# A decoder layer in float32 on one core: the fast-matmul block sums of both feed-forward layers reordered, and transfers regrouped where each turns to its second matmul

## The chip, the cores and the metric

One core of a Trainium2 chip runs the whole layer. The metric is device time in microseconds (us) of one execution; the time before is the median of three timed runs. One further execution was profiled, and its trace is what the rows below come from.

## What is computed

A decoder layer on 1024 tokens of width 1024, all in float32: a gated feed-forward layer, two attentions side by side, a second gated feed-forward layer, and a gated embedding. Only the feed-forward layers matter here. Cut to them:

```
def swiglu(h, w_gate, w_up, w_down):
    return (silu(h @ w_gate) * (h @ w_up)) @ w_down

x = x + 0.5 * swiglu(rms_norm(x, ffn1_norm), ffn1_w_gate, ffn1_w_up, ffn1_w_down)
...
x = x + 0.5 * swiglu(rms_norm(x, ffn2_norm), ffn2_w_gate, ffn2_w_up, ffn2_w_down)
```

The hidden width is 2816.

## The kernel before

**Precision.** A float32 operand is split into a rounded part "hi" (a cast on ScalarE, L102) and a remainder "lo" (a subtraction on VectorE, L103); `split` records both. A matmul of two such operands is three passes: hi by hi, hi by lo, lo by hi. So a product of 128 x 512 outputs over 512 inputs is 12 matmuls on TensorE, four a pass, and its second pass needs the lo of the activations, its third the lo of the weights.

**The first matmul of a feed-forward layer** (`ffn`) runs over 22 weight blocks n, gate and up in turn, of 256 hidden columns. Block 0 is multiplied in the plain way (`plain`, L251, 24 matmuls for each of 2 x 2 outputs). From n = 1 on, seven products take the place of eight (Winograd's scheme): tokens are halved into `N[0]` and `N[1]`, features into two halves, and the activations are the blocks B[1], B[2] (tokens of `N[0]`), "12" and B[3] (tokens of `N[1]`). The scheme needs four block sums of them: B[5] = "12" - B[1], called T1; B[6] = B[3] - B[5], called T2; B[7] = B[3] - "12", called T3; B[4] = B[2] - B[6]. Each is built in four tiles q of 128 tokens:

- `combo_a(q)` (L363) transposes tile q of `N[1]` on TensorE, copies it to a work tile `w` (L373, L374) and splits it into "12" and B[3].
- `combo_t(q)` (L379) makes T3, T1 and T2 of tile q with four subtractions on VectorE (L387 to L390) and splits T1 into B[5].
- `combo_s(q, m)` splits T2 into B[6] (m = 6) or T3 into B[7] (m = 7).
- `combo_d(q)` (L402) makes the sum for B[4] with two operations on GpSimd (L405, L406); `combo_e(q)` splits it.

`prep(n, m)` splits the weight operand of product (n, m), `sums` and `last_sum` make the weight sums on GpSimd (L268 to L273), `product` records the 12 matmuls (L300), `evict` moves the result.

**The order** is written out by hand. Inside `ffn` a manual schedule is on: every engine executes its instructions in the order of the code, so an instruction that waits holds up all that stand behind it on its engine. `first_entry` and `second_entry` order the start of the two layers, and both end in `products`; then comes the list `seqn`: (1,5), (2,1), (1,6), (2,2), (1,7), (2,6), (2,5), (1,4), (1,3), and so on. (1,5) needs all of B[5], (1,6) all of B[6], (1,7) B[7], (1,4) B[4].

**The first norm.** `first_entry` normalises the four tiles of `N[0]` one after the other: sum of squares (`norm_stat`, ScalarE, then two small operations on GpSimd, L181, L182), scaling (`norm_mul`, VectorE, L185), and transposes with splits (`norm_post`, TensorE, L190).

**The second matmul** (`down`, L494) adds 21 steps (c, i) of three chunks c, i = 0 to 6 being the seven products again. A step is 48 matmuls in the first chunk. Its operands come from DRAM through SyncE's queue: `load_hid(c, i)` loads a sum of the hidden values (two transfers of 512 KB, tile names GF and RN, KH and KL, or Q and Q in turn), `wd_block` loads weights, `load_resid` loads the residual rows X, in two halves of four transfers each. `prep_down(c, i)` splits both operands into four H tiles (four hold two steps), and `evict_down` adds the result to X on VectorE (L499). `prep_down(c, 1)` loads half of the next chunk's weights (names WH, and RAW or WL). "The turn" below is the passage from the first matmul to the second.

Of the kernel before, what the change touches and what calls it, by code (L numbers as in the profile page):

```python
# [35 lines left out]
def tile_hybrid_decoder_layer(  # L36
# [176 lines left out]
    def ffn(N, wg, wu, wd, next_gain, resid, hid, tags, entry, tail):  # L213
# [37 lines left out]
        def plain(f_, half):  # L251

            ps = bank(("pt", "pf")[f_])
            i = 0
            for kh in range(2):
                hl, rb = hls[0, ((1, 2), (5, 4))[f_][kh]], B[("12", 3)[kh]] if half else N[0]["B"][kh]
                for a, b in ((0, 0), (0, 1), (1, 0)):
                    for k in range(4):
                        pe(nc.tensor.matmul(ps[:], hl[:, a, k, :], right(rb, b, k), start=(i == 0), stop=(i == 23)))
# [3 lines left out]
            nc.scalar.activation(E[0][f_][:, half, :], ps[:], AF.Silu)
# [94 lines left out]
            nc.sync.dma_start(hid[j, :, 5:7, :], s34[:])  # L358
            del E[n], E[n - 1]

        C = {"w": {}, "t3": {}}

        def combo_a(q):  # L363

            h = N[1]["h"][q]
            cs = slice(q * P, (q + 1) * P)
            if q == 0:
                B[1], B[2] = N[0]["B"]
                B[3] = [slot("T", [P, 2, 512], F32R) for _ in range(4)]
                B["12"] = slot("X", [P, 2, 4, 512], F32R)  # L370
            w = C["w"][q] = slot(tags["w"][q], [P, 2, 4, P])
            v12, v22 = (turn(h, b, bank(cyc("t", ("pf", "av", "pf", "sc")))) for b in range(2))
            nc.scalar.copy(w[:, 0], v12)  # L373
# [4 lines left out]

        def combo_t(q):  # L379

            cs = slice(q * P, (q + 1) * P)
# [5 lines left out]
            nc.vector.tensor_sub(t3, w[:, 1], w[:, 0])  # L387
            nc.vector.tensor_sub(w[:, 0], w[:, 0], f(B[1][:, 0, :, cs]))
            nc.vector.tensor_sub(w[:, 0], w[:, 0], f(B[1][:, 1, :, cs]))
# [12 lines left out]

# [674 lines left out]
    def first_entry(F):  # L1077
# [13 lines left out]
        for t in range(4):
            norm_stat(N[0], t, ("PT", "WL")[t % 2])
            if t:
                norm_mul(N[0], t - 1)
                norm_post(N[0], t - 1, ps2)
# [12 lines left out]
        F["plain"](0, 0)
        F["a"](0)
        norm_mul(N[1], 2)  # L1110
        norm_mul(N[1], 3)
        F["a"](1)
        products(F)

    def products(F):
# [2 lines left out]
        F["prep"](1, 1)
        F["plain"](1, 0)
        F["a"](2)  # L1120
        F["prep"](1, 2)
# [7 lines left out]
        F["t"](1)
        F["s"](0, 7)  # L1130
        F["s"](1, 7)
        F["d"](0)
# [190 lines left out]
```

## Time and profile before

| | us |
|---|---|
| median of 3 runs | 2404.04 (2401.22 to 2408.77) |
| profiled execution | 2400.58 |
| its span | 2398.9 |
| TensorE busy in it | 2298.9 (96%) |
| VectorE, ScalarE, GpSimd busy | 1463.7, 983.9, 872.1 |
| TensorE busy in 0 to 20 | 5.88 |
| TensorE busy in 60 to 80 | 10.46 |
| TensorE busy in 500 to 520 | 14.51 |
| TensorE busy in 1660 to 1680 | 6.79 |
| TensorE busy in 2100 to 2120 | 14.11 |

In a row of the timeline stand: start, length from the start of the first to the end of the last, engine, line, operation, output and input tiles, form, count, and in brackets the idle time of the engine just before with what ended it. PE is TensorE, DVE VectorE, ACT ScalarE, POOL GpSimd, SPq the queue of SyncE that issues transfers. In a row of the waits stand the waiting engine and line, what it waited for, the sum in us, how often, and the longest. The granted clock (PEclk) is a share of TensorE's full speed. Tile names in the profile lack numbers, so many rows read "H" or "PT".

### The profile page before, as it was taken

To read this page: it belongs to the slowest core of one execution; us is meant where nothing else is said; L and a number is where in the kernel's file an instruction comes from. 1 tells how busy PE (TensorE), PEld (TensorE's weight loads), DVE (VectorE), ACT (ScalarE), POOL (GpSimd) and SP (SyncE) were. 2 spreads that over 40 slices of the span, in tenths; PEclk is the share of its full clock that TensorE was granted. 3 is DMA by queue.
4 is the path that set the end of the run, shared out by engine and by line. 5 is a ranking of instruction groups with operands and counts; after the bars stand their busy time and mean duration, and the time that the engine had idled before them with its cause. 6 is when DMAs were issued, how large, how long until landed. Compare 5 with 4: busy or idle time off the path is not lost.

```text
span 2398.9 us, 32295 instructions
## 1 busy us (share of the span) xinstructions
PE 2298.9 (96%) x12238; PEld 1972.5 (82%) x12238; DVE 1463.7 (61%) x2171; ACT 983.9 (41%) x1753; POOL 872.1 (36%) x752
## 2 busy tenths in 40 slices
PE   6899999989999999999988989997999999989999
PEld 5688888878888999988877877896888888878899
DVE  6754545577773656655665576547555455767763
ACT  5433333333352556544544554334333333333441
POOL 3444535300043556544454343104354453300031
PEclk9899999999999999999999999998999999999999
DMA  4222323373332122322213344432232332654232
GB/s 141 75 99 99 128 79 123 138 298 121 132 115 71 50 75 80 84 63 60 71 50 108 127 133 130 129 123 79 97 119 92 106 116 91 232 221 145 82 121 73
DMA packets 197500, 268.52 MB, mean 112 GB/s; under 512 B 27352, under 2 KB 130776, under 8 KB 197344
## 3 DMA queue, kind: packets, MB, share of 16 engines
q1 hardware_dynamic: 197344, 266.45, 33.3%
q8 instruction: 96, 1.57, 0.3%
q14 instruction: 60, 0.49, 0.1%
HBM read 188.78 MB, written 69.24 MB: 108 GB/s over the span
## 4 chain that ended last, share of the span: by engine, by line
PE 82%; DVE 8%; DMA 4%; ACT 2%; issue 2%; POOL 0%; SPq 0%; DVEq 0%; ACTq 0%; POOLq 0%
PE ps L300 33%; PE ps L494 13%; PE ps L595 11%; PE ps L603 9%; PE ps L1199 4%; PE ps L1051 3%; PE ps L876 3%; PE ps L858 2%; DVE H L103 1%; DVE RN L838 1%; PE ps L820 1%; PE ps L819 1%; DMA RN<-hidden 1%; DMA Q<-hidden 1%; DMA WL<-in_ffn_w_down_dram 1%
## 5 line engine op out<-in xcount | busy, mean ns | idle before, releaser
L494 PE MATMUL ps<-H,H 128*128 128x512 f32 x1848 | 427.6, 393 | 12.9 <-ACT H L102 11.4
L494 PEld LDWEIGHTS ps<-H,H 128*128 128x128 f32 x1848 | 349.6, 190 | 88.2 <-ACT H L102 13.1
L300 PE MATMUL ps<-H,WL 128*128 128x512 f32 x1008 | 243.4, 393 | 0.0
L300 PEld LDWEIGHTS ps<-H,WL 128*128 128x128 f32 x1008 | 189.7, 188 | 42.5
L603 PE MATMUL ps<-H,WH 128*128 128x512 f32 x768 | 212.8, 405 | 5.5 <-ACT PT L749 2.7
L129 POOL TENSOR_TENSOR WL<-RAW,WH 128x512 fp32r<-128x512 f32 (+1 forms) x112 | 130.4, 1188 | 167.7 <-ACT WH L123 129.8
L595 PE MATMUL ps<-WH,H 128*128 128x256 f32 (+1 forms) x1152 | 164.5, 285 | 4.0 <-DVE X L103 3.1
L603 PEld LDWEIGHTS ps<-H,WH 128*128 128x128 f32 x768 | 139.0, 191 | 30.0 <-ACT PT L749 2.9
L595 PEld LDWEIGHTS ps<-WH,H 128*128 128x128 f32 x1152 | 148.1, 189 | 6.2 <-DVE X L103 3.8
L129 POOL TENSOR_TENSOR WL<-Y,WH 128x528 fp32r<-128x528 f32 (+1 forms) x8 | 11.1, 1418 | 378.8 <-PE ps L494 189.6
L103 DVE TENSOR_TENSOR PT<-ps,PT 128x512 fp32r<-128x512 f32 (+1 forms) x160 | 100.4, 633 | 74.9 <-ACT PT L102 74.2
L300 PE MATMUL ps<-H,Q 128*128 128x512 f32 x600 | 143.4, 389 | 0.0
L499 DVE SCALAR_TENSOR_TENSOR X<-ps,X 128x512 f32<-128x512 f32 x168 | 109.0, 684 | 52.8 <-PE ps L494 52.8
L102 ACT CAST PT<-ps 128x512 fp32r<-128x512 f32 (+1 forms) x160 | 87.0, 546 | 111.7 <-PE ps L858 101.5
L300 PEld LDWEIGHTS ps<-H,Q 128*128 128x128 f32 x600 | 112.6, 188 | 24.0
L353 POOL TENSOR_TENSOR PT<-GF,RN 128x512 f32<-128x512 f32 x20 | 32.7, 1636 | 271.7 <-issue 147.0
L300 PE MATMUL ps<-H,PT 128*128 128x512 f32 x408 | 102.9, 404 | 26.0 <-ACT H L102 26.0
L876 PE MATMUL ps<-PT,X 128*128 128x256 f32 (+1 forms) x640 | 106.7, 285 | 20.0 <-DVE PT L103 19.7
L300 PE MATMUL ps<-X,WL 128*128 128x512 f32 x504 | 123.2, 393 | 0.0
L876 PEld LDWEIGHTS ps<-PT,X 128*128 128x128 f32 x640 | 95.9, 191 | 32.7 <-DVE PT L103 22.4
L300 PEld LDWEIGHTS ps<-H,PT 128*128 128x128 f32 x408 | 79.6, 196 | 44.3 <-ACT H L102 26.8
L839 POOL TENSOR_TENSOR T<-T,RN 128x127 f32<-128x127 f32 (+3 forms) x64 | 94.7, 1480 | 54.2 <-DVE RN L838 52.3
(367 smaller groups left out, 5082.4 us busy)
## 6 DMA issues: line engine op xcount, KB each, us to landing
WH<-in_ffn_w_gate_dram SPq DMA_DIRECT2D x40, 512.0 KB, 5.3
hidden<-PT SPq DMA_DIRECT2D x40, 512.0 KB, 3.0
KH<-in_ffn_w_up_dram SPq DMA_DIRECT2D x22, 512.0 KB, 5.9
hidden<-RN SPq DMA_DIRECT2D x22, 512.0 KB, 2.6
Q<-hidden SPq DMA_DIRECT2D x22, 512.0 KB, 7.2
RAW<-in_w_in_dram SPq DMA_DIRECT2D x22, 512.0 KB, 4.5
KL<-in_ffn_w_up_dram SPq DMA_DIRECT2D x20, 512.0 KB, 6.5
T<-in_ffn_w_down_dram SPq DMA_DIRECT2D x20, 512.0 KB, 4.4
```

The costliest lines, as they stand in the source:

```text
L102: a = nc.scalar.copy(hi, src) if eng_hi is nc.scalar else eng_hi.tensor_copy(hi, src)
L103: b = eng_lo.tensor_sub(lo, src, f(hi))
L129: ins = eng_lo.tensor_sub(lo[part], raw[part], f(hi[part]))
L300: pe(nc.tensor.matmul(ps[:], hl[:, a, k, :], rhs(m, b, k), start=(first and i == 0), stop=(final and i == 11), skip_group_check=True))
L494: pe(nc.tensor.matmul(groups[g][t][:], act[:, a, k, t * P:(t + 1) * P], wt[:, b, k, :], start=(fresh and n == 0), stop=(i in (6, 1, 4) and ...
L499: nc.vector.scalar_tensor_tensor(xs, groups[g][t][:], 0.5, xs, ALU.mult, ALU.add)
L595: pe(nc.tensor.matmul(ps[:, :n], hT[t // 4][a][:, k, (t % 4) * P:(t % 4 + 1) * P], w[k // 4][b][:, k % 4, :n], start=(i == 0), stop=(i == ...
L603: pe(nc.tensor.matmul(ps[:], w[a][:, k, :], hT[half][b][:, k, :], start=(i == 0), stop=(i == 23)))
L839: nc.gpsimd.tensor_mul(T[:, :n - 1], T[:, :n - 1], R[:, :n - 1])
L876: pe(nc.tensor.matmul(o, lh, r, start=(kpair == c and i == 0), stop=(kpair == 0 and i == 3)))
L1051: pe(nc.tensor.matmul(ps[:], w[a][:, k, :], yT[g][b][:, k, half * 512:half * 512 + 512], start=(i == 0), stop=(i == 11)))
L1199: pe(nc.tensor.matmul(ps[:, :256], mg[half][k // 2][a][:, k % 2, col:col + P], w[k // 4][b][:, k % 4, :], start=(i == 0), stop=(i == 23)))
```

## The change

1. **Block sums.** `combo_t` makes only T1, in a slot of its own (RN for the first two tiles, GF for the others), with two subtractions, and splits it. A new step `combo_u(q)` makes T3 and T2 in the work tile. `products` runs all four `combo_t` before any `combo_u`, B[6] after that, and the four `combo_s(q, 7)` with `combo_d(q)` at the very end. `combo_e` moves from behind the products 1 to 4 of `seqn` to behind 3 to 6.
2. **First norm.** `first_entry` runs `norm_stat` and `norm_mul` of a tile ahead of `norm_post` of the tile before.
3. **Transposes.** `plain` can be recorded in two halves of 12 matmuls; `combo_a` stands between the halves, and its transposes use more PSUM banks.
4. **The turn.** `load_resid(1)` moves from step 0 to step 1, behind `load_hid(0, 3)`; the next chunk's weights are loaded in `prep_down(c, 3)`, no longer in `prep_down(c, 1)`.

```
-            v12, v22 = (turn(h, b, bank(cyc("t", ("pf", "av", "pf", "sc")))) for b in range(2))
+            v12, v22 = (turn(h, b, bank(cyc("t", ("pf", "av", "pf", "sc", "pt", "av", "pt", "sc")))) for b in range(2))
...
-            w, t3 = C["w"][q], C["t3"][q // 2][:, q % 2]
-            nc.vector.tensor_sub(t3, w[:, 1], w[:, 0])
-            nc.vector.tensor_sub(w[:, 0], w[:, 0], f(B[1][:, 0, :, cs]))
-            nc.vector.tensor_sub(w[:, 0], w[:, 0], f(B[1][:, 1, :, cs]))
-            nc.vector.tensor_sub(w[:, 1], w[:, 1], w[:, 0])
-            split(B[5][:, 0, :, cs], B[5][:, 1, :, cs], w[:, 0], nc.scalar, nc.vector)
+            w, t1 = C["w"][q], C["t1"][q // 2][:, q % 2]
+            nc.vector.tensor_sub(t1, w[:, 0], f(B[1][:, 0, :, cs]))
+            nc.vector.tensor_sub(t1, t1, f(B[1][:, 1, :, cs]))
+            split(B[5][:, 0, :, cs], B[5][:, 1, :, cs], t1, nc.scalar, nc.vector)
+
+        def combo_u(q):
+
+            w, t1 = C["w"][q], C["t1"][q // 2][:, q % 2]
+            nc.vector.tensor_sub(w[:, 0], w[:, 1], w[:, 0])
+            nc.vector.tensor_sub(w[:, 1], w[:, 1], t1)
...
-                if i == 1:
+                if i == 3:
                     wd_block(c + 1, 0, 0, ("WH", "WH"))
...
-                if 0 < s < 5:
-                    combo_e(s - 1)
+                if 2 < s < 7:
+                    combo_e(s - 3)
...
+                if s == 1:
+                    load_resid(1)
                 if s == 0:
-                    load_resid(1)
```

On VectorE, at the start of the first layer behind the splits of the last tile, before: Q and KH are work tiles, RN is T3, H_408 is B[5], H_101 is B[1], X_439 is B[7].

```order
L387 TENSOR_TENSOR RN_409<-Q_273 128x512
L388 TENSOR_TENSOR Q_273<-Q_273,H_101 128x512
L389 TENSOR_TENSOR Q_273<-Q_273,H_101 128x512
L390 TENSOR_TENSOR Q_273<-Q_273 128x512
L103 TENSOR_TENSOR H_408<-Q_273,H_408 128x4x128
L103 TENSOR_TENSOR PT_416<-KH_114,PT_416 128x512
L325 TENSOR_TENSOR Y_405<-Y_405,ps_419 128x512
L387 TENSOR_TENSOR RN_409<-Q_294 128x512
L388 TENSOR_TENSOR Q_294<-Q_294,H_101 128x512
L389 TENSOR_TENSOR Q_294<-Q_294,H_101 128x512
L390 TENSOR_TENSOR Q_294<-Q_294 128x512
L103 TENSOR_TENSOR H_408<-Q_294,H_408 128x4x128
```

The same place in the changed kernel: RN and GF are T1, H_407 is B[5].

```order
L391 TENSOR_TENSOR RN_408<-Q_245,H_101 128x512
L392 TENSOR_TENSOR RN_408<-RN_408,H_101 128x512
L103 TENSOR_TENSOR H_407<-RN_408,H_407 128x4x128
L391 TENSOR_TENSOR RN_408<-Q_292,H_101 128x512
L392 TENSOR_TENSOR RN_408<-RN_408,H_101 128x512
L103 TENSOR_TENSOR H_407<-RN_408,H_407 128x4x128
L103 TENSOR_TENSOR PT_417<-KH_114,PT_417 128x512
L329 TENSOR_TENSOR Y_404<-Y_404,ps_420 128x512
L391 TENSOR_TENSOR GF_434<-KH_330,H_101 128x512
L392 TENSOR_TENSOR GF_434<-GF_434,H_101 128x512
L103 TENSOR_TENSOR H_407<-GF_434,H_407 128x4x128
```

A tile of B[5] is now three operations on VectorE and not five; the lo of its split stands right behind the subtraction whose result ScalarE has to cast first.

On GpSimd, at the same start, before: L268 to L273 are weight sums, L405 and L406 make the sum for B[4], of which H_102 is B[2].

```order
L273 TENSOR_TENSOR KL_115<-KL_115,RAW_368 128x4x128
L405 TENSOR_TENSOR Q_273<-H_102,Q_273 128x512
L406 TENSOR_TENSOR Q_273<-Q_273,H_102 128x512
L405 TENSOR_TENSOR Q_294<-H_102,Q_294 128x512
L406 TENSOR_TENSOR Q_294<-Q_294,H_102 128x512
L268 TENSOR_TENSOR RAW_487<-WH_313 128x512
L269 TENSOR_TENSOR WH_313<-WH_313,WH_314 128x4x128
L270 TENSOR_TENSOR RAW_487<-WH_313 128x512
L405 TENSOR_TENSOR KH_346<-H_102,KH_346 128x512
L406 TENSOR_TENSOR KH_346<-KH_346,H_102 128x512
```

The same in the changed kernel, with L272 to L277 the weight sums and L412, L413 the sum for B[4]:

```order
L277 TENSOR_TENSOR KL_115<-KL_115,RAW_387 128x4x128
L277 TENSOR_TENSOR WH_314<-WH_314,RAW_478 128x4x128
L412 TENSOR_TENSOR Q_245<-H_102,Q_245 128x512
L413 TENSOR_TENSOR Q_245<-Q_245,H_102 128x512
L412 TENSOR_TENSOR Q_292<-H_102,Q_292 128x512
L413 TENSOR_TENSOR Q_292<-Q_292,H_102 128x512
L412 TENSOR_TENSOR KH_330<-H_102,KH_330 128x512
L413 TENSOR_TENSOR KH_330<-KH_330,H_102 128x512
L412 TENSOR_TENSOR KL_365<-H_102,KL_365 128x512
L413 TENSOR_TENSOR KL_365<-KL_365,H_102 128x512
```

The eight operations for B[4] now stand in one block, behind both `last_sum` operations (L277), the second of which needs `prep(2, 2)`.

On SyncE's queue, at the first layer's turn, before: Q is the operand of step 2, GF and RN that of step 3, KH and KL (loads) that of step 4, X the residual, WH and WL the next chunk's weights.

```order
L457 DMA Q_3313<-hidden_91 128x2x512
L537 DMA X_3315<-in_x_dram 128x1024 x4
L431 DMA WH_3331<-in_ffn_w_down_dram 128x2x512
L431 DMA WH_3333<-in_ffn_w_down_dram 128x2x512
L431 DMA WL_3335<-in_ffn_w_down_dram 128x2x512
L431 DMA WL_3337<-in_ffn_w_down_dram 128x2x512
L537 DMA X_3316<-in_x_dram 128x1024 x4
L357 DMA hidden_91<-KH_3403 128x1024
L358 DMA hidden_91<-KL_3404 128x1024
L457 DMA GF_3425<-hidden_91 128x2x512
L457 DMA RN_3427<-hidden_91 128x2x512
L457 DMA KH_3485<-hidden_91 128x2x512
```

And in the changed kernel:

```order
L464 DMA Q_3313<-hidden_91 128x2x512
L544 DMA X_3315<-in_x_dram 128x1024 x4
L361 DMA hidden_91<-KH_3391 128x1024
L362 DMA hidden_91<-KL_3392 128x1024
L464 DMA GF_3413<-hidden_91 128x2x512
L464 DMA RN_3415<-hidden_91 128x2x512
L544 DMA X_3316<-in_x_dram 128x1024 x4
L464 DMA KH_3477<-hidden_91 128x2x512
L464 DMA KL_3479<-hidden_91 128x2x512
L438 DMA WH_3491<-in_ffn_w_down_dram 128x2x512
```

Eight transfers, four of X and four of weights, now stand behind the operand of step 3 and not ahead of it.

More of the change, by code (lines that the diff above doesn't have):

```diff
@@ L249, in part, with plain @@
             return {1: r[0][:, :, one], 5: r[0][:, :, two], 2: r[1][:, :, one], 3: r[1][:, :, one], 4: r[1][:, :, two]}[m]
[L251 to L255, printed above, removed]
+        def plain(f_, half, parts=(0, 1)):
+            if parts[0] == 0:
+                bank_of["plain"] = bank(("pt", "pf")[f_])
+            ps = bank_of["plain"]
+            i = 12 * parts[0]
+            for kh in parts:
                 hl, rb = hls[0, ((1, 2), (5, 4))[f_][kh]], B[("12", 3)[kh]] if half else N[0]["B"][kh]
@@ L260, in plain @@
                         i += 1
+            if i < 24:
+                return
             if 0 not in E:
@@ L359, in hidden_sums @@
             del E[n], E[n - 1]
-        C = {"w": {}, "t3": {}}
+        C = {"w": {}, "t1": {}}
         def combo_a(q):
@@ L397, in combo_s @@
                 B[m] = slot("H" if m == 6 else "X", [P, 2, 4, 512], F32R)
-            src = C["w"][q][:, 1] if m == 6 else C["t3"][q // 2][:, q % 2]
-            split(B[m][:, 0, :, cs], B[m][:, 1, :, cs], src, nc.scalar, nc.vector)
+            split(B[m][:, 0, :, cs], B[m][:, 1, :, cs], C["w"][q][:, 7 - m], nc.scalar, nc.vector)
         def combo_d(q):
@@ L514, in ffn @@
         with tc.manual_schedule():
-            entry(dict(a=combo_a, t=combo_t, s=combo_s, d=combo_d, load=load, prep=prep, sums=sums, last_sum=last_sum, plain=plain, product=lambda n, m: evict(n, m, product(n, m))))
+            entry(dict(a=combo_a, t=combo_t, u=combo_u, s=combo_s, d=combo_d, load=load, prep=prep, sums=sums, last_sum=last_sum, plain=plain, product=lambda n, m: evict(n, m, product(n, m))))
             for s, (n, m) in enumerate(seqn):
                 evict(n, m, product(n, m))
-                if 0 < s < 5:
-                    combo_e(s - 1)
+                if 2 < s < 7:
+                    combo_e(s - 3)
                 if s + LA < len(seqn):
@@ L1090, in first_entry @@
         F["load"](1)
[L1091 to L1095, printed above, removed]
+        norm_stat(N[0], 0, "PT")
+        norm_stat(N[0], 1, "WL")
+        norm_mul(N[0], 0)
+        norm_stat(N[0], 2, "WL")
+        norm_mul(N[0], 1)
+        norm_post(N[0], 0, ps2)
+        norm_stat(N[0], 3, "PT")
+        norm_mul(N[0], 2)
+        norm_post(N[0], 1, ps2)
         norm_mul(N[0], 3)
+        norm_post(N[0], 2, ps2)
         F["prep"](0, 1)
+        norm_post(N[0], 3, ps2)
         F["prep"](0, 2)
-        norm_post(N[0], 3, ps2)
         norm_stat(N[1], 0, "PT")
@@ L1104, in first_entry @@
         F["prep"](0, 4)
+        F["plain"](0, 0, (0,))
+        F["a"](0)
         norm_mul(N[1], 1)
@@ L1107, in first_entry, with products @@
         norm_stat(N[1], 3, "GF")
-        F["plain"](0, 0)
-        F["a"](0)
+        F["plain"](0, 0, (1,))
+        F["a"](1)
         norm_mul(N[1], 2)
         norm_mul(N[1], 3)
-        F["a"](1)
-        products(F)
-    def products(F):
+        products(F, (2, 3))
+    def products(F, rest=()):
         F["load"](2)
[L1118 to L1121, printed above, removed]
+        for i in range(2):
+            F["plain"](1, 0, (i,))
+            for q in rest[i:i + 1]:
+                F["a"](q)
+            F["prep"](1, 1 + i)
         F["sums"](1)
-        F["a"](3)
-        F["last_sum"](1)
         F["product"](1, 1)
         F["t"](0)
+        F["t"](1)
         F["prep"](1, 5)
         F["product"](1, 2)
[L1129 to L1132, printed above, removed]
         F["t"](2)
+        F["t"](3)
         F["plain"](0, 1)
-        F["d"](1)
-        F["t"](3)
-        F["prep"](2, 1)
+        F["u"](0)
+        F["u"](1)
         F["s"](0, 6)
         F["s"](1, 6)
-        F["d"](2)
+        F["prep"](2, 1)
         F["plain"](1, 1)
-        F["d"](3)
+        F["u"](2)
+        F["u"](3)
         F["s"](2, 6)
         F["s"](3, 6)
+        F["last_sum"](1)
         F["prep"](1, 6)
-        F["s"](2, 7)
-        F["s"](3, 7)
         F["prep"](2, 2)
-    tags = {"raw": {1: ("KH", "KL")}, "sum": {}, "w": ("Q", "Q", "KH", "KL"), "t3": "RN", "hl": ("WL", "WL", "WL", "WH") + ("PT",) * 4 + ("WL", "WL", "WL", "PT")}
+        for q in range(4):
+            F["s"](q, 7)
+            F["d"](q)
+    tags = {"raw": {1: ("KH", "KL")}, "sum": {}, "w": ("Q", "Q", "KH", "KL"), "hl": ("WL", "WL", "WL", "WH") + ("PT",) * 4 + ("WL", "WL", "WL", "PT")}
     X, N = ffn(N, ffn1_w_gate, ffn1_w_up, ffn1_w_down, mix_norm[0], x[0], ad[0], tags, first_entry, mix_start())
@@ L1240, in second_entry @@
         F["a"](1)
+        F["plain"](0, 0, (0,))
+        norm_mul(N[1], 3)
         F["prep"](0, 4)
-        norm_mul(N[1], 3)
-        F["plain"](0, 0)
+        F["a"](2)
+        F["plain"](0, 0, (1,))
+        F["a"](3)
         products(F)
@@ L1287, in tile_hybrid_decoder_layer @@
     tail, w = ple_start()
-    tags = {"raw": {0: ("RAW", "RAW"), 1: ("WH", "WH"), 2: ("RAW", "RAW"), 3: ("KH", "KH")}, "sum": {1: "WH", 2: "KL", 3: "KL"}, "w": ("Q", "Q", "KH", "KH"), "t3": "KL", "hl": ("WL", "WL", "WL", "KL") + ("PT",) * 4 + ("WL", "WL", "WL", "PT")}
+    tags = {"raw": {0: ("RAW", "RAW"), 1: ("WH", "WH"), 2: ("RAW", "RAW"), 3: ("KH", "KH")}, "sum": {1: "WH", 2: "KL", 3: "KL"}, "w": ("Q", "Q", "KH", "KH"), "hl": ("WL", "WL", "WL", "KL") + ("PT",) * 4 + ("WL", "WL", "WL", "PT")}
     ffn(N, ffn2_w_gate, ffn2_w_up, ffn2_w_down, ple_norm[0], xm, ad[1], tags, second_entry, tail)
```

2 lines of the change are left out of this document (1 added, 1 removed).

## The prediction

> **What bounds the kernel now.** The page first: TensorE is busy for nearly all of the span, so only what it waits for can be won. Then the waits of TensorE, by line and releaser:
>
> ```profile
> PE 2298.9 (96%) x12238; PEld 1972.5 (82%) x12238; DVE 1463.7 (61%) x2171; ACT 983.9 (41%) x1753; POOL 872.1 (36%) x752
> ```
>
> ```profile
> PE ps L300 <- ACT H L102: 26.0, 2, 13.8
> PE ps L494 <- ACT H L102: 11.4, 2, 5.9
> PE ps L190 <- DVE PT L185: 10.8, 2, 8.1
> PE ps L190 <- DVE WL L185: 5.3, 2, 2.7
> PE ps L494 <- DVE X L499: 1.5, 2, 0.8
> ```
>
> Of 100 us idle, 26 are two waits for B[5] (L300), 13 are waits at the two turns (L494), 8 stand between the first norm's tiles (L190, without the first 8.1, which nothing here touches). Those are what the change can reach. The timeline of TensorE places them: first layer, second layer, the two turns.
>
> ```profile
> 54.40 2.95 PE L259 MATMUL ps<-T,WH 128*128 128x512 f32 x12
> 69.54 7.93 PE L300 MATMUL ps<-H,PT 128*128 128x512 f32 x24 [12.19 <-ACT H L102]
> ...
> 88.36 1.98 PE L300 MATMUL ps<-H,WL 128*128 128x512 f32 x8
> ```
>
> ```profile
> 1673.21 8.23 PE L300 MATMUL ps<-H,PT 128*128 128x512 f32 x24 [13.78 <-ACT H L102]
> ...
> 1697.84 2.96 PE L300 MATMUL ps<-T,WL 128*128 128x512 f32 x12
> ```
>
> ```profile
> 470.27 30.08 PE L494 MATMUL ps<-H,H 128*128 128x512 f32 x132
> ...
> 508.56 14.02 PE L494 MATMUL ps<-H,H 128*128 128x512 f32 x48 [5.49 <-ACT H L102]
> 523.31 22.02 PE L494 MATMUL ps<-H,H 128*128 128x512 f32 x96 [0.73 <-DVE X L499]
> ...
> 2112.92 13.96 PE L494 MATMUL ps<-H,H 128*128 128x512 f32 x48 [5.89 <-ACT H L102]
> ```
>
> A matmul costs 22.02/96 = 0.23 us, a product of twelve 2.78. The 24 behind the B[5] wait take 7.93 where 5.56 would do, and the 48 behind a turn's wait 14.0 where 11.0 would: these waits leave TensorE slow for a while, worth 2.3 and 3.0 us.
>
> **The turns.** What ends the wait there is a landing (the L494 wait is for the split of GF):
>
> ```profile
> 485.01 1.05 ACT L102 CAST H<-Q 128x1024 fp32r<-128x1024 f32 x1 [10.64 <-DMA Q<-hidden]
> 486.29 1.05 ACT L102 CAST H<-Q 128x1024 fp32r<-128x1024 f32 x1 [0.23 <-DMA Q<-hidden]
> ...
> 505.34 1.04 ACT L102 CAST H<-GF 128x1024 fp32r<-128x1024 f32 x1 [16.10 <-DMA GF<-hidden]
> ```
>
> Two transfers of 512 KB land 1.28 apart. Eight now stand behind GF and RN: 10.2 earlier, so GF is cast at 495.1, after step 1 has freed its H tiles (470.27 + 2 x 11.0 = 492.3). Its four casts of 1.04 end at about 499.2; TensorE wants them at 508.56 - 5.49 = 503.1. Four us are spare, and the wait goes. Next late could be VectorE's add to X, which holds the other wait (0.73 here, 1.5 in both layers): its queue moves up with the splits by more than that. The second half of X lands four transfers behind RN, at about 496.4 + 4 x 1.28 = 501.5, and step 3 first adds to it at about 506. The weights of the next chunk are issued some 20 us later and used at step 6's start, 470.3 + 6 x 11.0 = 536: costs nothing, covered by 25 us. Worth 5.49 + 0.73 + 3.0 = 9.2 in the first layer and 5.89 + 0.77 + 2.9 = 9.6 in the second: 18.8.
>
> **The entries: what replaces the wait.** Rows of VectorE, ScalarE and GpSimd there:
>
> ```profile
> 45.68 0.68 DVE L387 TENSOR_TENSOR RN<-Q 128x512 f32<-128x512 f32 x1
> 46.40 0.69 DVE L388 TENSOR_TENSOR Q<-Q,H 128x512 f32<-128x512 f32 x1
> ...
> 60.98 1.64 DVE L389 TENSOR_TENSOR KH<-KH,H 128x512 f32<-128x512 f32 x1
> ...
> 75.93 1.28 DVE L103 TENSOR_TENSOR X<-RN,X 128x512 fp32r<-128x512 f32 x2
> ...
> 1649.37 0.68 DVE L387 TENSOR_TENSOR KL<-Q 128x512 f32<-128x512 f32 x1
> ```
>
> ```profile
> 30.71 1.28 ACT L263 ACT_TABLE_LOAD   x1
> ...
> 62.65 0.62 ACT L102 CAST H<-KH 128x512 fp32r<-128x512 f32 x1 [7.03 <-DVE KH L389]
> ```
>
> ```profile
> 31.87 1.26 POOL L268 TENSOR_TENSOR RAW<-KH 128x512 f32<-128x512 f32 x1
> ...
> 60.48 1.59 POOL L269 TENSOR_TENSOR WH<-WH,WH 128x512 f32<-128x512 f32 x1
> 62.15 1.60 POOL L270 TENSOR_TENSOR RAW<-WH 128x512 f32<-128x512 f32 x1
> ```
>
> Alone, VectorE takes a subtraction in 0.72 (46.40 - 45.68, one waiting for the other) or 0.60 (two in 1.28), but in 1.64 beside GpSimd's tensor operations, which grow from 1.26 to 1.6, and 1.67 from start to start: the two run in turns. That rate prices the change.
>
> Let t0 be VectorE's first subtraction for B[5], 45.7 before. A tile of B[5]: two subtractions 1.44, a wait for ScalarE's cast 0.65 (the old order covered it with the T2 subtraction), the lo 0.6: 2.7, four tiles 10.8; with `prep(1,5)` and an eviction 1.2, and one GpSimd sum in the way 1.0: 13.0. Then u and B[6] of two tiles with one `prep`, 4 x 0.72 + 3 x 0.6 = 4.7, twice 9.4; `prep(2,2)` 0.6. Here, at t0 + 23, GpSimd may start: `last_sum` and eight sums for B[4], 9 x 1.65 = 14.8. The last cast takes 0.6, and its lo stands behind up to five more operations on VectorE, 2.6 to 3.6 by how long GpSimd still runs. So the second pass of (1,4), which needs B[4]'s lo, may start at t0 + 41 to 42, and (1,3) 1.85 later (eight matmuls).
>
> TensorE is sooner: in the first layer B[5] is there at 45.4 + 13 = 58.4, its casts at 57.6, just as `plain` ends (before: 54.40 + 2.95 = 57.35). So the 12.2 go, and the slow clock with them; seven products later, with waits of about 1.7 each for `prep(2,1)` and for B[6]'s last tile, it would be at (1,4) around 82, and waits twice there, about 1.75 for hi and 2.7 for lo. (1,3) starts at 45.4 + 43.5 = 88.9; before, two products behind the row at 88.36, at 93.9: 5.0 won of 14.5.
>
> In the second layer the third and fourth transposes are copied earlier, but `prep(1,2)`'s cast now stands behind the activation that ends `plain(1,0)`; I put t0 at 1647.1, 2.3 ahead of 1649.37, with bounds of 0 and 4. (1,3) starts at 1647.1 + 42.6 = 1689.7, before at 1697.84: 8.1 won of 16.
>
> **The first norm and the transposes.** Of 8.0 (three waits) 2.5 remain, as the scaling now has a tile's lead and waits for VectorE's splits alone; `plain(0,0)` starts 5.5 sooner. It reaches t0 by no more than 0.3 (45.4 for 45.7): the third tile of `N[1]` is scaled on VectorE behind the splits of `combo_a(1)`, and these wait for ScalarE, which first does two sums of squares, the table load (1.28, at 30.71 before), an activation and copies. So TensorE would stand idle ahead of those transposes, for some 4 us, most of the 5.5 that it had gained. (1,3) hangs on t0, so only the 0.3 counts; bounds 3 sooner to 1.5 later.
>
> **A slow clock in the new waits.** After a short gap:
>
> ```profile
> 764.31 5.25 PE L603 MATMUL ps<-H,WH 128*128 128x512 f32 x16 [2.05 <-DVE KL L677]
> ```
>
> and the stretch behind it in the view by windows (the last three numbers are the granted clock, the share of the DMA engines, GB/s):
>
> ```profile
> 764.30:767.00 2.70, 2.69 (x6) 2.13 (x7) 1.39 (x2) 0.00 (x0) 0.00 (x0) 0.50 0.94 244
> ```
>
> Sixteen matmuls take 5.25 for 3.7: a gap of 2.05, near others, halves the granted clock (0.50) and costs 1.5. The pair of gaps in (1,4) is as long, so I charge 1.5 in each layer, 3.0; bounds 0 and 6.0. [...]
>
> **Sum.** 2400.58 - 18.8 - 5.0 - 8.1 + 3.0 = 2371.7 on the profiled execution, which was 3.5 under the median: 2375.2 on the median.
>
> **Rivals.**
> - *Faster entries*: GpSimd's block costs VectorE less than rows say. At 1.26 each it ends 3 sooner, the lo follows at once (3 more), and no clock is lost: 7 a layer, 2361. Against it: each pair of rows from 57 to 63 runs in turns. 0.13.
> - *Entries that win nothing*: t0 late by 1.5, clock lost two or three times a layer, some waits more: 2404 - 19 = 2385. For it: five new short gaps in each layer. 0.14.
> [...]
> - *The turns keep their wait*: something other than the eight transfers holds GF (its slot, or the sums written ahead of it). Then only entries win: 2394. Against it: landings follow at 1.28 all through. 0.05.
> - *Slower*: the block for B[4] ends so late that (1,4) waits more than the old B[5] did. It decides once the nine operations take over 14.8 and all that the layer wins: 14.8 + 5.0 + 9.2 - 1.5 = 27.5 in the first, 14.8 + 8.1 + 9.6 - 1.5 = 31.0 in the second, 3.1 and 3.4 each; at 4 each, 2375 + 2 x 9 x 2.35 = 2417. The longest of this size take 1.7. 0.03.
> - The forecast, 0.56; 0.03 for turns and entries both winning nothing.
>
> That the code does something else is out: the order shows all four parts.
>
> **Range and chances.** Known bounds: turns 16 to 19, the gains of entries from 0 to 27 with the clock. 2362 to 2386 leaves out the last two rivals, the even case and ends: under 2 in 10. A measurement tells 0.3% (7 us). Faster: 0.56 + 0.13 + 0.14 + 0.06 + 0.05 = 0.94; same 0.03; slower 0.03.
>
> **What would show it.** Right: no L300 wait for B[5] above 1 us, but two waits at (1,4) (hi, then lo) just behind eight L412/L413 rows of some 1.6 each; VectorE rows of 1.6 beside them; GF cast near 10 us earlier, and no wait in step 3 or 4; about 4 us of idle TensorE before the third transposes at 32 to 36. Wrong: any L494 wait at the turns over 1; (1,3) in the first layer before 86 or after 92; L412 rows at 1.3.

## The result and the profile after

The changed kernel takes 2376.94 us in the median of four runs (2376.4 to 2379.38); the kernel before, 2402.63 beside it. The ratio is 0.9892, with a 95% interval of 0.9871 to 0.9913: faster by 1.1%, and inside the predicted range (2362 to 2386, forecast 2375). The profiled execution took 2376.99, its span 2375.2, against 2398.9 before.

TensorE's busy time and its waits, by line and releaser, in the changed kernel (L304 was L300, L501 was L494):

```profile
PE 2296.6 (97%) x12238; PEld 1969.5 (83%) x12238; DVE 1462.2 (62%) x2171; ACT 985.5 (41%) x1753; POOL 873.8 (37%) x752
```

```profile
PE ps L304 <- DVE X L103: 5.3, 4, 2.8
PE ps L190 <- DVE WH L185: 5.0, 1, 5.0
PE ps L304 <- ACT X L102: 3.9, 2, 1.9
...
PE ps L304 <- ACT WL L102: 3.1, 2, 1.6
```

The two long waits for B[5] are gone, and so are all waits of the down products: no row of L501 is left. In their place stand a 5.0 ahead of the third transposes of `N[1]` (L190, first layer), and waits for B[4] and the splits around it. The timeline of TensorE at (1,4) and (1,3) of the first layer, and the first down products (the count in brackets is the idle time before the row):

```profile
36.43 1.97 PE L190 MATMUL ps<-identf,WH 128*128 128x128 f32 x8 [4.97 <-DVE WH L185]
...
86.12 1.19 PE L304 MATMUL ps<-X,WL 128*128 128x512 f32 x4 [1.94 <-ACT X L102]
90.12 3.78 PE L304 MATMUL ps<-X,WL 128*128 128x512 f32 x8 [2.81 <-DVE X L103]
93.70 3.52 PE L304 MATMUL ps<-T,WL 128*128 128x512 f32 x12
97.06 2.89 PE L304 MATMUL ps<-X,Q 128*128 128x512 f32 x12
...
470.66 89.69 PE L501 MATMUL ps<-H,H 128*128 128x512 f32 x395
```

At 97.06 stands the product that stood at 96.67 before:

```profile
96.67 2.89 PE L300 MATMUL ps<-X,Q 128*128 128x512 f32 x12
```

So the first layer's entry has won nothing. At the turn the down products run through without a gap, and the first cast of GF, at 505.34 before, stands here:

```profile
495.64 1.05 ACT L102 CAST H<-GF 128x1024 fp32r<-128x1024 f32 x1 [5.96 <-DMA GF<-hidden]
```

To see where the rest went, cut the span at rows that every kernel has: A to the first down product, B to the last one, C to the last rows of the output projection, 1.5 us before its end (attention and mixture, whose instructions no kernel here changes), D to the second layer's first down product, E to its last, F the rest.

| us | A | B | C | D | E | F |
|---|---|---|---|---|---|---|
| before | 470.3 | 223.6 | 933.1 | 447.2 | 224.1 | 100.6 |
| changed | 470.7 | 214.0 | 932.7 | 443.2 | 214.1 | 100.5 |
| difference | +0.4 | -9.6 | -0.4 | -4.0 | -10.0 | -0.1 |

So 19.6 of 23.7 us come from the two turns (B and E), and 4.0 from the second entry (D).

### The profile page after: what moved, and what is told of

Same layout as the page of the kernel before. It is cut to its first block, busy times and chain, and to the rows that moved or that the text cites. A ratio compares the mean times of both kernels' runs of the same rounds, so it can differ in the third digit from the quotient of the medians.

```text
span 2375.2 us, 32326 instructions
## 1 busy us (share of the span) xinstructions
PE 2296.6 (97%) x12238; PEld 1969.5 (83%) x12238; DVE 1462.2 (62%) x2171; ACT 985.5 (41%) x1753; POOL 873.8 (37%) x752
## 4 chain that ended last, share of the span: by engine, by line
PE 86%; DVE 8%; ACT 3%; issue 2%; DMA 1%; POOL 0%; SPq 0%; DVEq 0%; ACTq 0%; POOLq 0%
PE ps L304 32%; PE ps L501 17%; PE ps L603 11%; PE ps L611 9%; PE ps L1212 4%; PE ps L1059 3%; PE ps L884 3%; PE ps L866 2%; PE ps L828 1%; PE ps L827 1%; DVE RN L846 1%; PE ps L190 1%; DVE X L103 1%; DVE RN L844 1%; DVE PT L103 1%
## 5 line engine op out<-in xcount | busy, mean ns | idle before, releaser
L501 PE MATMUL ps<-H,H 128*128 128x512 f32 x1848 | 420.9, 389 | 0.0
L501 PEld LDWEIGHTS ps<-H,H 128*128 128x128 f32 x1848 | 346.4, 188 | 71.7
L304 PE MATMUL ps<-H,WL 128*128 128x512 f32 x1008 | 243.6, 393 | 3.1 <-ACT WL L102 3.1
L304 PEld LDWEIGHTS ps<-H,WL 128*128 128x128 f32 x1008 | 189.6, 188 | 46.4 <-ACT WL L102 4.0
L304 PE MATMUL ps<-H,Q 128*128 128x512 f32 x600 | 143.4, 389 | 0.0
L129 POOL TENSOR_TENSOR WL<-Y,WH 128x528 fp32r<-128x528 f32 (+1 forms) x8 | 11.1, 1416 | 359.2 <-PE ps L501 359.2
L304 PE MATMUL ps<-X,WL 128*128 128x512 f32 x504 | 128.3, 402 | 10.2 <-DVE X L103 5.3
L304 PEld LDWEIGHTS ps<-H,Q 128*128 128x128 f32 x600 | 112.6, 188 | 24.0
L304 PEld LDWEIGHTS ps<-X,WL 128*128 128x128 f32 x504 | 96.3, 193 | 34.9 <-DVE X L103 7.0
L611 PE MATMUL ps<-H,WL 128*128 128x512 f32 x384 | 108.6, 404 | 0.0
```

What stands on the lines that cost most here:

```text
L129: ins = eng_lo.tensor_sub(lo[part], raw[part], f(hi[part]))
L304: pe(nc.tensor.matmul(ps[:], hl[:, a, k, :], rhs(m, b, k), start=(first and i == 0), stop=(final and i == 11), skip_group_check=True))
L501: pe(nc.tensor.matmul(groups[g][t][:], act[:, a, k, t * P:(t + 1) * P], wt[:, b, k, :], start=(fresh and n == 0), stop=(i in (6, 1, 4) and ...
L611: pe(nc.tensor.matmul(ps[:], w[a][:, k, :], hT[half][b][:, k, :], start=(i == 0), stop=(i == 23)))
```

## The experiments

All but the first are edits of the changed kernel. The stages of the profiled executions, as differences from the changed kernel, with the medians of four runs each (ten for entries_only) and the ratios to the kernel before in the same session:

| run | A | B | C | D | E | median | ratio (interval) |
|---|---|---|---|---|---|---|---|
| turn_only | +0.2 | 0.0 | +7.6 | +3.8 | 0.0 | 2387.04 | 0.9933 (0.9918 to 0.9948) |
| entries_only | -0.8 | +9.5 | +3.6 | -1.2 | +9.9 | 2397.93 | 0.9983 (0.9973 to 0.9992) |
| d_vector | -3.0 | +0.1 | +2.3 | -3.6 | +1.5 | 2370.87 | 0.9872 (0.9858 to 0.9887) |
| mul_ahead | -3.3 | 0.0 | -0.3 | -1.1 | -0.1 | 2372.56 | 0.9882 (0.9865 to 0.9898) |
| order_27 | -3.5 | +0.1 | +2.7 | +0.8 | -0.1 | 2376.87 | 0.9894 (0.9879 to 0.9909) |
| fill_wait | -2.3 | 0.0 | +3.2 | -2.6 | -0.1 | 2373.67 | 0.9883 (0.9869 to 0.9898) |
| old_norm | +4.6 | 0.0 | +2.7 | 0.0 | 0.0 | 2383.34 | 0.9922 (0.9907 to 0.9937) |
| both | -7.8 | +0.1 | -1.0 | -4.9 | -0.1 | 2366.53 | 0.9854 (0.9838 to 0.9871) |
| no_halves | -3.2 | 0.0 | +4.2 | +4.0 | 0.0 | 2380.59 | 0.9907 (0.9891 to 0.9924) |
| mixed | -5.8 | +0.1 | +0.3 | -3.3 | -0.1 | 2367.66 | 0.9859 (0.9844 to 0.9874) |
| both_27 | -11.1 | +1.7 | 0.0 | -2.7 | -0.1 | 2364.84 | 0.9856 (0.9840 to 0.9873) |
| cover | -14.1 | +0.1 | +2.4 | -3.7 | 0.0 | 2360.65 | 0.9833 (0.9818 to 0.9848) |

C moves by up to 8 us though nothing in it is edited; the last section shows that it is the clock (granted 0.98 where C took 940.3, 0.99 before). An edit is therefore judged by A, B, D and E first, and by the median second. These stages move too where nothing in them is edited, but less: D by 1.2 in entries_only and by 1.1 in mul_ahead, E by 1.5 in d_vector, B by 1.7 in both_27. A holds the kernel's start as well: in `both` the last transposes of the first norm ended at 17.25 and not at the 18.10 of the changed kernel, and the first transposes of `N[1]` came 0.8 sooner than there (21.82 for 22.62). So 1 to 2 us in one stage of one execution say little.

**The turn alone, and the entries alone.** turn_only puts these two edits into the kernel before; entries_only takes them out of the changed one.

```
-                if i == 1:
+                if i == 3:
                     wd_block(c + 1, 0, 0, ("WH", "WH"))
...
+                if s == 1:
+                    load_resid(1)
                 if s == 0:
-                    load_resid(1)
```

> The kernel before with nothing but the later residual and chunk loads at the turn. My account of the two traces (spans 2398.9 and 2375.2) gives the turns 9.9 us in the first layer and 10.1 in the second, 20.0 in all, and that the entries add to this without touching it: 2402.6 - 20.0 = 2382.6, ratio 0.9917. Rival (the entries carry most of it, and the turn only gains because the entries shift it): 2395 or more. Rival in the other direction (the turn carries all): 2377. In its trace: no wait in the line of the down products at the two turns, the first GF cast some 10 us ahead of 505.3.

> The changed kernel with the old places of the residual and chunk loads. By the account the entries are worth -0.4 us in the first layer and 4.1 in the second: 2402.6 - 3.7 = 2398.9, ratio 0.9985, with both waits of 5.5 and 5.9 back at the turns. The prediction's own terms (3.5 and 6.6 after its clock charge) would give 2392.5. Rival: 2385 or less, if the two parts only gain together.

B and E are 9.6 and 10.0 shorter with the turn edit, whatever stands in the entries, and as long as before without it. entries_only came out at 2397.93, 4.3 faster than before, as expected. turn_only came out at 2387.04, 4.4 slower than expected: its own stages do what they should, but in the profiled execution (2388.56) its C took 940.3. So the parts add up in the stages that they touch.

**The old norm.** The first norm of the first layer back in its old order, one tile after the other.

```
-        norm_stat(N[0], 0, "PT")
-        norm_stat(N[0], 1, "WL")
-        norm_mul(N[0], 0)
-        norm_stat(N[0], 2, "WL")
...
+        for t in range(4):
+            norm_stat(N[0], t, ("PT", "WL")[t % 2])
+            if t:
+                norm_mul(N[0], t - 1)
+                norm_post(N[0], t - 1, ps2)
```

> The changed kernel with the first norm in its old order (scale, transpose, split of one tile after the other). The prediction says that its 5.5 us do not reach (1,3), since the path there goes over the splits of N[1]'s tiles: then the first plain product starts some 5.5 later, the idle of 5.0 ahead of the third transposes goes, and the time is 2377 to 2378. Rival (the norm carries through): 2382.

The prediction's claim falls: A is 4.6 longer, the median 6.4. The idle ahead of the third transposes did not shrink, it moved along (TensorE, then VectorE's first subtraction for B[5]):

```profile
41.91 1.97 PE L190 MATMUL ps<-identf,WH 128*128 128x128 f32 x8 [5.00 <-DVE WH L185]
```

```profile
52.50 0.68 DVE L391 TENSOR_TENSOR RN<-Q,H 128x512 f32<-128x512 f32 x1
```

The subtraction stands at 52.5, against 47.09 in the changed kernel and 45.68 before. The chain of tiles starts from the first plain product, which comes 5.9 later (23.80 for 17.92), so most of the norm's gain carries through: 5.4 to this subtraction, 4.6 to the end of A. And with the norm taken off, the rest of the edit has made this chain 6.8 longer.

**Scalings ahead of the splits.** VectorE's queue of the changed kernel there: it stands idle, takes the splits of the second tile in turns with GpSimd's sums (1.35 and 2.88 where 0.69 and 0.75 would do), and only then scales the third tile (L185). The last row is the first subtraction for B[5]:

```profile
31.03 1.35 DVE L103 TENSOR_TENSOR X<-Q,X 128x512 fp32r<-128x512 f32 x1 [3.52 <-ACT X L102]
32.30 2.88 DVE L103 TENSOR_TENSOR T<-Q,T 128x256 fp32r<-128x256 f32 x2
35.10 1.27 DVE L185 SCALAR_TENSOR_TENSOR WH<-X,rs,PT 128x1024 f32<-128x1024 f32 x1
...
47.09 0.68 DVE L391 TENSOR_TENSOR RN<-Q,H 128x512 f32<-128x512 f32 x1
```

```
+        norm_mul(N[1], 2)
+        norm_mul(N[1], 3)
         F["plain"](0, 0, (1,))
         F["a"](1)
-        norm_mul(N[1], 2)
-        norm_mul(N[1], 3)
```

> The changed kernel with the scalings of the third and fourth tiles of N[1] (first layer only) ahead of the splits of the second tile on VectorE. They need rs at 28.3 and 29.2, and VectorE stood idle from 27.5 to 31.0. The third transposes then follow the second half of the plain product at about 31.5 instead of 36.4 (5.0 us of TensorE idle go), and the first subtraction for B[5] comes 3 to 4 us ahead of 47.1. If everything up to (1,4) hangs on that subtraction, (1,3) comes as much sooner: 2377 - 3.5 = 2373.5. Rival (the B[4] block, or the landing of the next weights, holds (1,4) by itself): the idle only moves from the transposes to (1,4), 2377 and waits of 5 or more there.

The time is 2372.56, and A 3.3 shorter. The third transposes start at 31.74 without a wait, the first subtraction at 43.50, and (1,4) goes on 43.0 behind it, as in the changed kernel (90.12 - 47.09 = 43.0):

```profile
31.74 1.03 PE L190 MATMUL ps<-identf,WH 128*128 128x128 f32 x8
...
86.50 3.78 PE L304 MATMUL ps<-X,WL 128*128 128x512 f32 x8 [2.79 <-DVE X L103]
```

So (1,3) does hang on that subtraction; what was wrong is what sets it. TensorE now waits 3.48 ahead of product (1,1) instead of the 4.97 ahead of the transposes, and that wait holds up nothing on this path.

**Whole plain products.** The transposes of `N[1]` behind whole plain products in both layers, with the old scalings, splits and banks; the new norm stays. The edit, cut to its part in the first layer:

```
-        F["plain"](0, 0, (0,))
-        F["a"](0)
         norm_mul(N[1], 1)
...
-        F["plain"](0, 0, (1,))
-        F["a"](1)
+        F["plain"](0, 0)
+        F["a"](0)
         norm_mul(N[1], 2)
         norm_mul(N[1], 3)
+        F["a"](1)
```

> The changed kernel with the transposes of N[1] back behind whole plain products in both layers, in the old order of scalings, splits and banks; the pipelined norm, the order of the block sums and the turns stay. The run with the old norm lost 6.4, so the chain to the first subtraction for B[5] does hang on the first plain product, against the prediction. Then, before and after, that subtraction stood at 45.7 and 47.1 although the norm was 5.3 sooner in the second: the move between the halves must have cost the first layer some 6.5. Without it the subtraction should come at 41 to 43, the idle of 5.0 ahead of the third transposes go, and (1,3) come 4 to 6 sooner; in the second layer, where it is the only thing that moved the subtraction (2.2 sooner by the two traces), it should be 2.3 later. Sum 2377 - 5 + 2.3 = 2374. Rival (the sums of the next weights on GpSimd, which run beside the splits either way, hold the first layer): the subtraction stays at 46 to 47, and the time is 2379 to 2380.

The first layer is 3.2 shorter (the first subtraction at 42.22, expected 41 to 43; 4 to 6 were expected of (1,3)), the second 4.0 longer (expected 2.3). In the second layer B[5] is late again:

```profile
55.73 3.01 PE L304 MATMUL ps<-H,PT 128*128 128x512 f32 x12 [2.31 <-ACT H L102]
...
1655.53 7.57 PE L304 MATMUL ps<-H,PT 128*128 128x512 f32 x24 [3.52 <-ACT H L102]
```

As the edit has it, the move between the halves wins in the second layer and loses in the first. It is not the halves alone that lose there: mul_ahead keeps them and is as short in A. The median, 2380.59, was expected at 2374: 1.8 from the first layer, 1.7 from the second, and C at +4.2.

**The sums for B[4].** GpSimd's block in the first layer of the changed kernel, from its first operation to what follows it:

```profile
70.18 1.62 POOL L277 TENSOR_TENSOR WH<-WH,RAW 128x512 f32<-128x512 f32 x1 [21.25 <-issue]
71.76 1.75 POOL L412 TENSOR_TENSOR Q<-H,Q 128x512 f32<-128x512 f32 x1
...
83.82 1.59 POOL L413 TENSOR_TENSOR KL<-KL,H 128x512 f32<-128x512 f32 x1
85.38 1.73 POOL L272 TENSOR_TENSOR RAW<-KH 128x512 f32<-128x512 f32 x1
```

Nine operations take 15.2 (85.4 - 70.2), 23.1 behind the first subtraction. VectorE's splits beside them, and one of the same form behind them:

```profile
75.68 1.77 DVE L103 TENSOR_TENSOR WL<-RAW,WL 128x512 fp32r<-128x512 f32 x1
...
87.58 0.68 DVE L103 TENSOR_TENSOR WL<-KL,WL 128x512 fp32r<-128x512 f32 x1
```

d_vector puts the eight on VectorE:

```
-            nc.gpsimd.tensor_sub(w[:, 0], f(B[2][:, 0, :, cs]), w[:, 1])
-            nc.gpsimd.tensor_add(w[:, 0], w[:, 0], f(B[2][:, 1, :, cs]))
+            nc.vector.tensor_sub(w[:, 0], f(B[2][:, 0, :, cs]), w[:, 1])
+            nc.vector.tensor_add(w[:, 0], w[:, 0], f(B[2][:, 1, :, cs]))
```

> The changed kernel with the eight sums for B[4] on VectorE instead of GpSimd. If what holds (1,4) is that GpSimd and VectorE take turns there (15.2 us for nine GpSimd operations, VectorE's splits at 1.77 instead of 0.6), the eight take 8 x 0.7 = 5.6 on VectorE, its splits are back at 0.6, and B[4] is ready some 5 us sooner: both waits in (1,4) (1.94 and 2.81; 1.95 and 1.72) go, and the slow clock behind them (2.3 and 2.8), while (1,7) waits 1.5 to 2.5 for its own splits, which now stand behind the sums. Net 3 to 5 a layer: 2377 - 8 = 2369. Rival (VectorE's own load binds, not the turns): no gain, 2377, with the same waits in (1,4). GpSimd busy falls by some 26 us in all.

2370.87, with A 3.0 and D 3.6 shorter: the 3 to 5 a layer that were expected if the sums on GpSimd hold (1,4). The run takes away GpSimd's own slower rate (1.28 alone, at 92.06 in the changed kernel, for VectorE's 0.69) and the turns with VectorE together, so it does not tell the two apart. VectorE takes seven of the eight in 0.69 and one, beside GpSimd, in 1.67; (1,4) starts without a wait, and (1,7) waits as expected:

```profile
76.63 0.69 DVE L413 TENSOR_TENSOR KH<-KH,H 128x512 f32<-128x512 f32 x1
```

```profile
77.98 4.13 PE L304 MATMUL ps<-X,WL 128*128 128x512 f32 x8 [2.40 <-DVE X L103]
...
88.55 2.95 PE L304 MATMUL ps<-X,WL 128*128 128x512 f32 x12
```

**The slow clock behind the new waits.** Windows of the changed kernel right behind the waits of (1,4), first and second layer (the last three numbers are the granted clock, the share of the DMA engines, GB/s):

```profile
90.00:93.70 3.70, 3.58 (x9) 2.82 (x9) 0.67 (x2) 0.62 (x1) 1.56 (x2) 0.50 0.36 123
1680.00:1683.00 3.00, 3.00 (x8) 2.32 (x8) 0.36 (x1) 1.01 (x2) 0.95 (x1) 0.50 0.87 260
```

fill_wait lets TensorE multiply into a free bank while it would wait:

```
+                if (n, m) == (1, 4) and i in (0, 4):
+                    fill = bank("av")
+                    for k in range(7):
+                        pe(nc.tensor.matmul(fill[:], hl[:, 0, k % 4, :], rhs(5, 0, k % 4), ...))
```

> The changed kernel with seven matmuls of no use (into a free bank, never read) ahead of each of the two waits of (1,4), in both layers: 1.6 us of work in gaps of 1.7 to 2.8. If it is the gaps that halve the granted clock, TensorE now idles only 0.1 to 1.2, the clock stays at 1.0, and the 2.3 and 2.8 us lost at 0.50 behind them come back: 2377 - 5 = 2372, although work is added. Rival (the clock falls for another reason, such as the transfers that land just then, a share of 0.87 of the DMA engines at 1680 to 1683): 2377 or up to 1 later, with 0.50 still there.

With 28 matmuls more, the kernel is faster: 2373.67, A 2.3 and D 2.6 shorter, and each of its four runs is below all four of the changed kernel. The longest wait that is left in (1,4) is 1.17, and the granted clock of the same stretch (here the number before the DMA share) is 1.00:

```profile
87.07 1.79 PE L306 MATMUL ps<-H,WL 128*128 128x512 f32 x7
90.03 2.13 PE L308 MATMUL ps<-X,WL 128*128 128x512 f32 x8 [1.17 <-DVE X L103]
92.00 2.95 PE L308 MATMUL ps<-T,WL 128*128 128x512 f32 x12
```

```profile
90.00:93.70 3.70, 3.67 (x16) 1.00 0.36 125
```

The transfers are the same (0.36). In the second layer, where the changed kernel's window shows 0.50 at a share of 0.87, the eight and twelve matmuls behind the gaps take 2.13 and 2.96 in fill_wait, for 3.78 and 4.02. So it is the idle time. What it costs varies: behind the two gaps of the first layer, 1.94 and 2.81 in the changed kernel and 1.95 and 2.80 in no_halves, the next 8 and 12 matmuls took 3.78 and 3.52 in the one, 3.78 and 4.14 in the other. In the second layer the D of mul_ahead, which edits nothing there, is 1.1 shorter.

**A product ahead of (1,4).** order_27 moves (2,7):

```
-        seqn = [... (2, 6), (2, 5), (1, 4), (1, 3), (2, 7)]
+        seqn = [... (2, 6), (2, 5), (2, 7), (1, 4), (1, 3)]
```

> The changed kernel with product (2,7) ahead of (1,4) and (1,3), in both layers. If (1,4) hangs on the GpSimd block for B[4] and nothing else, one more product (2.75) ahead of it takes that much out of its two waits (4.75 and 3.67), and a part of the slow clock behind them (2.3 and 2.8) with it: 3 to 5 a layer, 2377 - 7 = 2370. Rival (the waits only move, since the splits for (2,7) and B[4] queue on the same VectorE): 2377, with the same sum of waits.

2376.87: nothing won in the median, where 7 was expected. A is 3.5 shorter, C 2.7 longer (TensorE busy 898.6 in it for 895.8); in the second layer the products up to (3,1) come 5.4 sooner, and then (3,7) waits. The rows of TensorE and ScalarE:

```profile
1703.51 5.49 PE L304 MATMUL ps<-X,Q 128*128 128x512 f32 x12 [3.21 <-ACT Y L324]
```

```profile
1702.36 0.62 ACT L102 CAST PT<-WH 128x512 fp32r<-128x512 f32 x1 [4.34 <-DMA WH<-in_ffn_w_gate_dram]
1702.88 0.58 ACT L324 COPY Y<-ps 128x512 f32<-128x512 f32 x1
```

(3,7) needs the bank of (3,6), whose copy (L324) stands on ScalarE behind the first cast of the next weights, and these land late. SyncE issues their load behind the stores of the hidden sums, 2.2 later than in the changed kernel (1697.87 for 1695.65). The wait and the 5.49 for 2.8 give back 5.9. The expectation of both_27, below, names (4,1) as the waiting product; it is (3,7).

**Together.** `both` is mul_ahead with the sums on VectorE, one tile at a time behind the splits of later products:

```
+                    for q in ((0,), (1,), (2, 3))[s] if s < 3 else ():
+                        combo_d(q)
```

> The changed kernel with the third and fourth scaling of N[1] ahead (as in the run before, which won 4.4), and the eight sums for B[4] on VectorE, now not between the splits of B[7] but one tile at a time behind the splits that (1,7), (2,6) and (2,5) need. If the run of turns between GpSimd and VectorE is the cause, no wait is left from (2,2) to (1,3) in either layer, and no 0.50 there: 3.6 for the scalings, 7 in the first layer and 6.5 in the second, 2377 - 17 = 2360. Rival (VectorE then is late with the splits of (1,7) to (1,4) instead, as in the run with the sums between the splits): 2366 to 2370.

2366.53, at the rival's end: (1,4) still waits 1.32 and 2.57 in the first layer, for splits in a queue of VectorE that has no gap from 61.9 to 83.5. With GpSimd out of the way, VectorE's own load binds. `mixed` takes the first layer's whole plain products instead of the scalings ahead:

> The eight sums for B[4] on VectorE behind the splits of the next products (as in the run called both), with the first layer's transposes behind whole plain products and the second layer's between the halves. The second layer should be that of both (4.8 ahead of the changed kernel from its entry to its first down product). In the first layer, if the old order of scalings and splits gives the first subtraction for B[5] sooner than 43.5, the first down product comes sooner than the 462.9 of both, by as much: 1 to 2.5, and the time is 2364 to 2366. Rival (GpSimd's sums of the weights meet the splits and hold the subtraction at 43.5 or later): 2367 or more.

2367.66, and its A is 2.0 longer than that of `both`: the rival's side. Its first subtraction came at 43.44. That of `both` came at 42.23, but with its early start; the other runs with the scalings ahead have it at 43.50 (mul_ahead), 43.25 (both_27) and 43.02 (cover). So the old order is no better than the scalings ahead, and not shown to be worse. both_27 is `both` with the order of order_27; `cover` also puts two tiles' subtractions ahead of their splits:

```
-            split(B[5][:, 0, :, cs], B[5][:, 1, :, cs], t1, nc.scalar, nc.vector)
+            for p in (q - 1, q) if q % 2 else ():
+                ps_ = slice(p * P, (p + 1) * P)
+                split(B[5][:, 0, :, ps_], B[5][:, 1, :, ps_], C["t1"][p // 2][:, p % 2], ...)
```

> The run called both (2366.5) with product (2,7) ahead of (1,4) and (1,3) as in order_27. Alone on the changed kernel this won 3.4 in the first layer, and 5.4 in the second, of which 6 were given back 20 us later: product (4,1) waited 3.2 for its weights and ran on at a granted clock of 0.5 to 0.8, since their loads stand on SyncE's queue behind the stores of the hidden sums, and these came 2.2 later from GpSimd. In both, (1,4) waits 1.32 and 2.57 in the first layer, 0.34 and 2.57 in the second: the product ahead of it takes the 2.57 and the slow clock behind (1.8 in the first). If the second layer gives it back again: 2362 to 2364, with a wait of 2 or more ahead of (4,1). If not, as GpSimd is free earlier there: 2360. Rival (VectorE, busy without a gap from 61.9 to 83.5, is as late for (1,4) whatever stands ahead, and later with the splits of (2,7)): 2366.

> The same as both_27, with the subtractions of two tiles of B[5] ahead of their two splits, so that VectorE no longer stands idle 0.69 for ScalarE's cast in each tile. If VectorE's queue is what (1,4) hangs on, two of the four idle spells are covered by the next tile's subtractions and the two others in part: 1.4 to 2.1 sooner in each layer, 3 to 4 us in all against both_27. Rival (after the two runs of sums moved, TensorE's products are late enough to hide VectorE): the same time as both_27 within 1.

both_27 takes 2364.84, a little over the 2362 to 2364 expected: A is 3.3 shorter than in `both`, D 2.2 longer, with (3,7) waiting 2.94 again. `cover` takes 2360.65, 4.2 less than both_27 (3 to 4 were expected; 3.0 of it is in A and 1.0 in D, where 1.4 to 2.1 each were expected), at a ratio of 0.9833 to the kernel before where the changed kernel has 0.9892. (1,4) hardly waits any more, in either layer:

```profile
81.03 2.12 PE L304 MATMUL ps<-X,WL 128*128 128x512 f32 x8 [0.19 <-DVE X L103]
...
1659.67 5.75 PE L304 MATMUL ps<-X,WL 128*128 128x512 f32 x24
```

What is left in the second layer is (3,7), at 3.58. Loading those weights ahead of the stores was not tried.

## Why the prediction was right, and where it was not

- **The turns** were right in mechanism and size: 19.6 for 18.8. GF is cast at 495.64, 9.7 earlier (10.1 with the later start), and neither the add to X nor the next weights came late. The two groups of transfers that moved, X and the weights, were not tested apart.
- **The second entry's start** was right: t0 at 1637.68 is 2.1 sooner than before, once the 9.6 of the first turn are added; 2.3 was forecast.
- **The entries' pattern** was right: no wait for B[5], 1.5 to 1.6 at (2,1) and (1,6) (the second ends with the cast of its weights, right behind that of B[6]'s last tile), then 1.94 and 2.81 at (1,4) for 1.75 and 2.7. GpSimd's nine took 15.2 for 14.8. d_vector shows that these sums on GpSimd are the cause; how much of it is the turns with VectorE, and how much GpSimd's own rate, is not shown.
- **The first entry's size** was wrong. (1,3) was forecast at 88.9, and after 92 was to count as wrong: it came at 93.70. Two terms failed. First, "t0 at 45.4": it came at 47.09. The prediction saw the 4 us of idle ahead of the third transposes (4.97 measured) and took them for slack that would swallow the norm's gain; old_norm shows that the norm is worth 4.6 in A and the rest of the edit there costs 5.0 against the kernel before, mul_ahead and no_halves that 3.2 to 3.3 of this is the new order of splits and scalings (no_halves moves the transposes and the banks too). Both were missed, and they nearly cancelled. Second, the way from t0 to (1,4)'s second pass: 43.0 in the first layer for 41 to 42, as GpSimd goes straight on with the next weights' sums (the row at 85.38) and VectorE stays slow (a split of 1.77 at 85.89). It was 41.9 in the second, where 40.8 had been put in.
- **The clock** was undersized in the first layer: 1.5 was charged, and fill_wait shows 2.3. In the second it shows 2.6 against the changed kernel and 1.5 against mul_ahead's D, so there the size is not settled. Without a charge the sum would be 2372; the 0.50 behind the waits speaks against that, the times alone could not tell 2372 from 2375.
- **A small slip**: 22.02/96 makes a product of twelve 2.75, not 2.78; no term moves by more than 0.1.

The entries thus won 3.6 where 10.1 were forecast after the clock's charge, the turns 0.8 more: on the profiled executions the sum missed by 5.3 (2376.99 for 2371.7). On the median it missed by 1.7, since the kernel before was profiled 3.5 under its median of then and the changed one at its median. Part of the closeness is luck.

## What to carry to other kernels

Idle time of the main engine ahead of a step is slack only if the step's inputs do not start from that engine's own earlier work; undo the edit before it to find out. Before sums go to an idle engine, look whether its operations run in turns with the busy one: here nine sums on GpSimd took 15.2 us, and VectorE's splits beside them went from 0.68 to some 1.78; eight of them took 6.5 on VectorE (1.67 and seven of 0.69). Where a wait cannot be removed, work of no use in it can pay: here it kept the clock at 1.00 where it had been 0.50, and the time was 2373.67 for 2376.94.

## What the runs showed of the hardware

The unedited stage C took 931.7 to 940.3 in fourteen profiled executions. TensorE's idle time in it is nearly the same (36.0 to 37.2 in ten of them), and the busy time of the same matmuls is not. Windows over that stage, before and turn_only (length, busy time, granted clock, share of the DMA engines, GB/s):

```profile
693.90:1626.80 932.90, 896.17 (x5713) 0.99 0.31 92
```

```profile
684.90:1625.10 940.20, 903.53 (x5714) 0.98 0.31 91
```

Idle is 36.7 in both (932.90 - 896.17, 940.20 - 903.53); so all of the 7.3 is busy time of the same matmuls, at a granted clock of 0.98 for 0.99. Which gaps slow the matmuls behind them is not settled, and their length alone does not tell. Behind 3.48 sixteen matmuls took 6.63 in both_27 (at 41.51) and 5.53 in cover (at 41.28, the same place). Behind 2.05 sixteen took 5.25 for 3.7 (at 764.31 before), but behind 2.31 twelve took 3.01 (no_halves, at 55.73), where an undisturbed product takes 2.88. Behind two gaps of 0.34 and 2.57, with 1.2 of work between them, the next 8 and 12 matmuls took 2.13 and 2.95 in the second layer of `both`; behind two of 0.36 and 2.57 they took 2.89 and 3.76 in that of mixed. So nearly the same gaps can cost time in one execution and not in another. What decides it, no run here shows.
